# Byte offsets of split weight tiles by kind of product, and a reordered start, in a two-block float32 model on one core

## The chip, the cores and the metric

The kernel runs on one NeuronCore of a Trainium2 chip. The metric is the device time of one execution in microseconds; lower is better. Before the change the median of three runs is 3207.17 us (3205.44 to 3207.61).

## What is computed

Two transformer-like blocks of width 1024 follow each other, each with two layers, in float32. The first block carries 256 latent and 256 context tokens; its layers hold two half-step swiglus and a mixer, Fourier in the first and retention in the second, and every part is modulated by shifts, scales and gates that are products of a condition vector with `ada_w`. The second block carries the 256 latent tokens alone, with a mixer of gated recurrences and attention. Cut to what matters:

```
def swiglu(h, w_gate, w_up, w_down):
    return (jax.nn.silu(h @ w_gate) * (h @ w_up)) @ w_down
def half_ffn(t, m, j):
    h = modulate(rmsnorm(t, norm_g[l, j]), m[3 * j], m[3 * j + 1])
    return t + 0.5 * m[3 * j + 2] * swiglu(h, ffn_w_gate[l, j // 2], ffn_w_up[l, j // 2], ffn_w_down[l, j // 2])
x = half_ffn(x, m_lat, 0)
h_lat = modulate(rmsnorm(x, norm_g[l, 1]), m_lat[3], m_lat[4])
x = x + m_lat[5] * y_lat
x = half_ffn(x, m_lat, 2)
```

The hidden width of a swiglu is 2816. In the second block a layer is x + 0.5 swiglu, x + mixer, x + 0.5 swiglu, and the mixer's input product has 10752 columns. In the last layer of the first block only the latent tokens are needed behind retention.

## The kernel before

**Split products.** A float32 product is made of three products of rounded parts: every operand is split into a high part (type fp32r) and a low part, and `mm3` (L272 to L274) issues high by high, high by low, low by high into one PSUM tile. Activations are kept split in SBUF (class `Split`, tiles `s`); weights are split as they arrive.

**Requests for weights.** Every use of a weight piece is one call of `get` or `getw` (L205, L222), a *request*. A first pass over the whole program with dummies writes the list of requests, the plan; the second pass emits instructions and looks ahead in that plan. `pump` (L176) issues the DMA of a request up to four requests ahead on SP (`_dma`, L150, into one of four `raw` buffers) and then its split (`_split`, L158): ScalarE copies the piece to `wh` (L166), VectorE makes `wl` = raw - `wh` (L167), both in tiles of a pool with three buffers. The subtraction is put off into `subs` and emitted at the next `tick`, or at the latest when its request is asked for. A piece has up to 2048 columns per partition: 8 k tiles of 256 columns, 4 of 512, or fewer.

**Offsets.** A `wh` or `wl` buffer is 512 bytes longer than its piece. Where `odd` is set, the tile starts at a byte offset that rotates with the number i of the request in the plan, the same for `wh` and `wl`:

```
o = OFFSETS[i % len(OFFSETS)] // 4 if odd else 0
```

with the 16 values 0, 4, 8, 12, 16, 20, 24, 28, 32, 40, 48, 56, 64, 96, 128 and 192. `odd` is set behind the first three swiglus, so retention and all that follows rotates, and what stands ahead has offset 0. Raw requests (`ada_n`, `ada_t`) count in i but are not split.

**Kinds of product.** The first two and a half layers multiply with 512 columns moving (both streams, `ffn2s`, L592), except each swiglu's first gate and up request, its last four k tiles (`by_stream`, L663) and the Fourier layer, which go stream by stream with 256 columns. Behind that nearly all have 256 columns moving and the weights stationary (`gemm_t`, L566): swiglus (`ffn`, L691), retention's q and gates, the mixers' transposed units (`unit_t`, L1223). Retention's k requests move 512 columns. The swiglu behind retention moves 258 in gate and up (`shift`). In `gemm_n` (L583) the activations are stationary and the weights move, 256 columns: retention's v and the mixers' `unit_n` (L1234).

**The order on the engines** is the order in which the Python code emits; nothing reorders it later. In the mixers, `tick` (L226) puts steps of attention and recurrence chains between the products.

**The start** (L1721 to L1746). `consts` (L360) loads vectors, the identity and the two halves of x on ScalarE's queue. `ada_first` (L392) makes the first shift and scale on TensorE from two times four raw chunks of `ada_n`. `sums` gathers squares of x (ScalarE L477, VectorE L483), `rstd` turns them into 1/rms, `lead` (L541) scales x by it, and `lead_end` (L551) applies scale and shift and splits: ScalarE L556 for the high part, VectorE L558 and L560 for the low. The first weight request stands before the last raw chunk. The first gate request runs on the latent half k tile by k tile, two output tiles each, with all three products at once (`pair_t`, L574, `early` 2).

Of the kernel before, what the change touches and what calls it, by code (L numbers as in the profile page):

```python
# [10 lines left out]
F32R = mybir.dt.float32r  # L11
# [8 lines left out]
KT = 8  # L20
# [8 lines left out]
LATE = 9  # L29
SCRATCH = 1024  # L30
GAP = 2048 - SCRATCH - 128
OFFSETS = (0, 4, 8, 12, 16, 20, 24, 28, 32, 40, 48, 56, 64, 96, 128, 192)
PAD = 512

# [55 lines left out]
class Ker:  # L90
    def __init__(self, tc, I, out, plan):
# [17 lines left out]
        self.uid = 0  # L109
        self.quiet = False  # L110
        self.splim = None
        self.odd = False

# [44 lines left out]
    def _split(self, i):  # L158
        src, raw, odd = self.plan[i]
# [5 lines left out]
        wl = self.wsp.tile([128, 2048 + PAD // 4], F32R, name="wl", tag="wl")[:, o:]  # L165
# [38 lines left out]

    def get(self, src, raw=False):  # L205
        self.asked.append((src, raw, self.odd))
# [4 lines left out]
        assert self.plan[i] == (src, raw, self.odd) or str(self.plan[i]) == str((src, raw, self.odd))  # L211
# [10 lines left out]
    def getw(self, w, k0, k1, c0, c1):  # L222
        return self.get(w.rearrange("(k p) m -> p k m", p=128)[:, k0:k1, c0:c1])

# [134 lines left out]
class Model(Ker):  # L359
    def consts(self):  # L360
# [10 lines left out]
        nc.scalar.dma_start(self.x[:, :, CTX], xv[:, :, CTX])  # L371
        self.late[LATE] = self.ada_begin
# [199 lines left out]


    def pair_t(self, ps, u, X, c, early):  # L574
        cut = [(k, k + 1) for k in range(KT)] if early == 2 else [(0, 6), (6, KT)] if early else [(0, KT)]
        for k0, k1 in cut:
# [15 lines left out]
    def ffn2s(self, H, wg, wu, wd, gate, g_next, mid=None, late=(0, 1, 4), first=None):  # L592
# [3 lines left out]
        def up(f0, f1):  # L596
            G = Gs[f0] = Split(self, f1 - f0, N1)
            for f in range(f0, f1, 2):
                ug = first if first and f == 0 else self.getw(wg, 0, KT, 128 * f, 128 * f + 256)
                pg = [self.mm() for _ in range(2)]  # L600
                if f == 0:
# [3 lines left out]
                    for c in STREAM:  # L605
                        for u, p in ((ug, pg), (uu, pu)):
                            for m in self.pair_t([p[m][:, c] for m in range(2)], u, H, c, 2 if first and u is ug and c == LAT else 0):
                                self.tick()
# [11 lines left out]
                uu = self.getw(wu, 0, KT, 128 * f, 128 * f + 256)  # L620
                for m in range(2):
# [6 lines left out]
        def down(f0, f1):  # L628
            G = Gs[f0]
            ks = ((f0, f0 + 5), (f0 + 5, f1)) if f1 - f0 > 8 else ((f0, f1),)  # L630
            for mp in range(4):
                pd = [self.mm() for _ in range(2)]
                for k0, k1 in ks:
                    u = self.getw(wd, k0, k1, 256 * mp, 256 * mp + 256)
                    for m in range(2):
# [55 lines left out]
    def ffn(self, X, wg, wu, wd, resid, after=None, shift=False):  # L691
        n = N2 + 2 if shift else N2
        cx, c = slice(0, n), slice(0, N2)
        for hi, (f0, f1) in enumerate(self.HALVES):
            G = Split(self, f1 - f0, N2)
            for f in range(f0, f1, 2):
                ug = self.getw(wg, 0, KT, 128 * f, 128 * f + 256)
# [3 lines left out]
                uu = self.getw(wu, 0, KT, 128 * f, 128 * f + 256)  # L701
                pu = [self.mm([128, n]) for _ in range(2)]
# [213 lines left out]
    def retention(self, H, before, after):  # L916
# [21 lines left out]
        for hd in range(4):  # L938
# [27 lines left out]
            uk = self.getw(wi, 0, KT, 1024 + 256 * hd, 1280 + 256 * hd)  # L966
            pk = [self.mm() for _ in range(2)]
# [745 lines left out]
def body(M, stop):  # L1713
# [15 lines left out]

    def load():  # L1730
        M.splim = LATE - 1
        first.append(M.getw(I["ffn_w_gate"][0, 0], 0, KT, 0, 256))
    H = Split(M, KT, N1)
    M.splim = LATE - 2
# [34 lines left out]

    M.odd = True  # L1770
    M.retention(H, lambda: M.shifted_begin(2), M.pre)
# [62 lines left out]
```

## Time and profile before

| | |
|---|---|
| median of three runs | 3207.17 us |
| the profiled execution's own time | 3207.72 us |
| its span | 3205.9 us |
| TensorE products busy | 3165.0 us, 99% |
| VectorE busy | 2192.3 us, 68% |
| ScalarE busy | 1367.3 us, 43% |
| DMA | 510.69 MB, mean 159 GB/s |

The rows further down come from this one execution. Times are microseconds from the start of the span; a row of a stretch gives its limits, its length, then for each engine the busy time and the number of instructions in it, the granted share of TensorE's clock (1.00 is 2.4 GHz) and what the DMA moved.

### The profile page before, as it was taken

The page shows a single profiled execution, that of the slowest core. Times are in us where ns is not written, and L with a number is a line of the kernel's source. Part 1 is how long each engine was busy: PE and PEld are TensorE (multiplying, and loading weights), DVE is VectorE, ACT ScalarE, POOL GpSimd, SP SyncE. Part 2 cuts the span into 40 slices and gives each one's busy share as a digit, 9 for nine tenths or more (in the row PEclk, how much of TensorE's full clock was granted, in tenths as well). Part 3 has the DMA queues.
Part 4 walks back from the last instruction along what each step waited for, and adds up shares of the span by engine and source line. Part 5 has one row for each costly group of instructions (what it writes and reads, how often), then busy time and mean ns, then how long its engine had stood idle before and what let it go on. Part 6 is the DMA issues. An engine that isn't in the chain of part 4 may idle for free.

```text
span 3205.9 us, 53822 instructions
## 1 busy us (share of the span) xinstructions
PE 3165.0 (99%) x22520; PEld 2968.3 (93%) x22520; DVE 2192.3 (68%) x4077; ACT 1367.3 (43%) x1945; POOL 0.5 (0%) x5
## 2 busy tenths in 40 slices
PE   7999999999999999999999999999999999999999
PEld 5888898888988889999999999999999999999999
DVE  6797578874666537666757568767757568876755
ACT  3222353222322225444445456654544446655543
POOL 0000000000000000000000000000000000000000
PEclk9999999999999999999999999999999999999999
DMA  7465413554256532333555554444565555444563
GB/s 266 168 220 181 140 54 132 184 197 131 80 175 218 170 103 94 118 113 124 166 178 194 186 176 158 146 144 132 191 191 185 183 172 175 145 147 142 172 195 122
DMA packets 431699, 510.69 MB, mean 159 GB/s; under 512 B 8800, under 2 KB 396128, under 8 KB 431456
## 3 DMA queue, kind: packets, MB, share of 16 engines
q1 hardware_dynamic: 426656, 501.25, 47.5%
q10 hardware_dynamic: 4800, 5.99, 0.6%
q8 instruction: 177, 2.90, 0.4%
q14 instruction: 66, 0.54, 0.0%
HBM read 506.16 MB, written 1.05 MB: 158 GB/s over the span
## 4 chain that ended last, share of the span: by engine, by line
PE 92%; DVE 5%; ACT 1%; DMA 1%; issue 1%; ACTq 0%; DVEq 0%
PE mm L272 30%; PE mm L274 29%; PE mm L273 29%; PE mm L1450 2%; DVE wl L167 1%; DMA x<-in_xT 1%; DVE x L658 1%; PE mm L1609 1%; DVE s L523 0%; PE aux L1659 0%; PE mm L1593 0%; DVE s L520 0%; DVE sqs L483 0%; PE mm L1641 0%; ACT wh L166 0%
## 5 line engine op out<-in xcount | busy, mean ns | idle before, releaser
L272 PE MATMUL mm<-s,wh 128*128 128x256 f32 (+2 forms) x5888 | 1829.3, 311 | 4.4 <-ACT s L521 2.5
L273 PE MATMUL mm<-s,wh 128*128 128x256 f32 (+2 forms) x5888 | 1820.8, 309 | 2.5 <-DVE s L1337 0.7
L274 PE MATMUL mm<-s,wl 128*128 128x256 f32 (+2 forms) x5888 | 1819.6, 309 | 2.3 <-DVE wl L167 2.3
L272 PEld LDWEIGHTS mm<-s,wh 128*128 128x128 f32 x5888 | 1114.7, 189 | 63.9 <-ACT s L521 3.7
L273 PEld LDWEIGHTS mm<-s,wh 128*128 128x128 f32 x5888 | 1114.5, 189 | 63.6 <-DVE s L523 3.9
L274 PEld LDWEIGHTS mm<-s,wl 128*128 128x128 f32 x5888 | 1114.4, 189 | 61.6 <-DVE wl L167 3.9
L167 DVE TENSOR_TENSOR wl<-raw,wh 128x2048 fp32r<-128x2048 f32 (+2 forms) x438 | 929.0, 2123 | 244.0 <-ACT wh L166 244.0
L166 ACT ACTIVATE wh<-raw 128x2048 fp32r<-128x2048 f32 (+2 forms) x438 | 776.3, 1778 | 612.9 <-PE mm L273 224.9
L457 DVE SCALAR_TENSOR_TENSOR jk<-raw,s 128x512 bf16<-128x512 f32 x448 | 309.0, 690 | 12.2
L272 PE MATMUL mm<-wh,s 128*128 128x256 f32 x960 | 275.8, 287 | 0.0
L273 PE MATMUL mm<-wl,s 128*128 128x256 f32 x960 | 269.9, 281 | 0.0
L274 PE MATMUL mm<-wh,s 128*128 128x256 f32 x960 | 269.9, 281 | 0.0
L752 ACT ACTIVATE s<-tmp 128x256 fp32r<-128x256 f32 (+1 forms) x176 | 87.8, 499 | 423.2 <-DVE tmp L738 319.6
L273 PEld LDWEIGHTS mm<-wl,s 128*128 128x128 f32 x960 | 181.9, 189 | 0.2
L272 PEld LDWEIGHTS mm<-wh,s 128*128 128x128 f32 x960 | 181.6, 189 | 0.3
L274 PEld LDWEIGHTS mm<-wh,s 128*128 128x128 f32 x960 | 181.6, 189 | 0.0
L738 DVE TENSOR_TENSOR tmp<-tmp,mm 128x512 f32<-128x512 f32 x66 | 45.2, 685 | 195.8 <-PE mm L274 158.7
L658 DVE SCALAR_TENSOR_TENSOR x<-mm,cm,x 128x256 f32<-128x256 f32 x160 | 71.8, 478 | 105.5 <-PE mm L274 105.5
L750 DVE TENSOR_TENSOR tmp<-mm,sqs 128x256 f32<-128x256 f32 x88 | 36.8, 418 | 83.1 <-PE mm L274 83.1
L754 DVE TENSOR_TENSOR s<-tmp,s 128x256 fp32r<-128x256 f32 (+1 forms) x176 | 91.3, 519 | 2.2 <-ACT s L752 1.1
L749 ACT ACTIVATE tmp<-tmp 128x256 f32<-128x256 f32 x88 | 36.2, 411 | 102.8 <-DVE tmp L748 102.8
L483 DVE TENSOR_TENSOR sqs<-sqs,tmp 128x256 f32<-128x256 f32 x119 | 49.8, 418 | 25.7 <-ACT tmp L477 24.6
(243 smaller groups left out, 1988.8 us busy)
## 6 DMA issues: line engine op xcount, KB each, us to landing
raw<-in_ffn_w_in SPq DMA_DIRECT2D x88, 1024.0 KB, 4.9
raw<-in_w_in SPq DMA_DIRECT2D x84, 1024.0 KB, 4.8
raw<-in_ada_t SPq DMA_DIRECT2D x64, 1024.0 KB, 5.3
raw<-in_ffn_w_gate SPq DMA_DIRECT2D x44, 1024.0 KB, 5.2
raw<-in_ffn_w_up SPq DMA_DIRECT2D x44, 1024.0 KB, 5.2
raw<-in_ret_w_in SPq DMA_DIRECT2D x24, 1024.0 KB, 4.9
raw<-in_ffn_w_out SPq DMA_DIRECT2D x32, 768.0 KB, 4.6
raw<-in_ffn_w_down SPq DMA_DIRECT2D x32, 640.0 KB, 4.0
```

What stands on the lines that cost most here:

```text
L166: self.A.activation(wh[:, :n], t[:, :n], AF.Copy)
L167: self.subs.append((i, lambda: self.V.tensor_sub(wl[:, :n], t[:, :n], wh[:, :n].bitcast(F32))))
L272: T.matmul(ps, ah, bh, start=first, stop=False)
L273: T.matmul(ps, ah, bl, start=False, stop=False)
L274: T.matmul(ps, al, bh, start=False, stop=last)
L457: V.scalar_tensor_tensor(jk, r[:, j, 512 * i:512 * i + 512], 1.0, self.cb[s][i], OP.mult, OP.mult, accum_out=a[:, 2 * q + j, s, i:i + 1])
L483: self.defer(lambda: self.V.tensor_add(sqs, sqs, q))
L658: self.V.scalar_tensor_tensor(self.x[:, d, e], ps[:, e.start - c.start:e.stop - c.start], gate(d, s), self.x[:, d, e], OP.mult, OP.add)
L738: V.tensor_mul(g, sg, pu)
L752: A.activation(G.h(f), g, AF.Copy)
L754: self.defer(lambda: V.tensor_sub(G.l(f), g, G.h(f).bitcast(F32)))
L1450: T.matmul(ps[:m, a, b], kc, qc, start=True, stop=True)
```

## The change

The rotation and the flag `odd` go. Each request names its offset: `NARROW` (64 bytes) is the default of `getw`, `WIDE` (0) is given where 512 columns move, `MOVING` (192) in the mixers' `unit_n`; retention's v keeps the default. The gate and up requests of the swiglu behind retention take the 22 values of `SHIFTED` in turn. The early layers' narrow requests so change from 0 to 64. The buffers are as long as before.

At the start, x is loaded on SP ahead of the chunks, in the order latent, context. The sums and scalings of both halves move between the chunks of `ada_n` (`latent` and the other hooks), the first weight request comes behind the last chunk, and its low part is not emitted when it is asked for (`lazy`), but by `catch_up` behind `lead_end`. Its latent half runs in three passes over all k tiles, high by high, high by low, low by high (`pair_first`). The core of the diff:

```
-        o = OFFSETS[i % len(OFFSETS)] // 4 if odd else 0
-        wh = self.wsp.tile([128, 2048 + PAD // 4], F32R, name="wh", tag="wh")[:, o:]
+        wh = self.wsp.tile([128, 2048 + PAD // 4], F32R, name="wh", tag="wh")[:, at // 4:]
...
+WIDE, NARROW, MOVING, PAD = 0, 64, 192, 512
+SHIFTED = (12, 68, 72, 76, 80, 84, 52, 44, 204, 200, 208, 196, 140, 136, 132, 144, 40, 36, 100, 88, 160, 176)
...
+    def getw(self, w, k0, k1, c0, c1, at=NARROW):
...
-        if self.subs and self.subs[0][0] <= i:
+        if self.subs and self.subs[0][0] <= i and not self.lazy:
...
-        nc.scalar.dma_start(self.x[:, :, LAT], xv[:, :, LAT])
+        for c in STREAM:
+            nc.sync.dma_start(self.x[:, :, c], xv[:, :, c])
...
+    def pair_first(self, ps, u, X, c):
+        wh, wl = u
+        for i in range(3):
+            for k in range(KT):
+                x = (X.l if i == 1 else X.h)(k, c.start, c.stop)
+                for m in range(2):
+                    self.T.matmul(ps[m], (wh, wh, wl)[i][:, k, 128 * m:128 * m + 128], x,
+                                  start=i == 0 and k == 0, stop=i == 2 and k == KT - 1)
...
+                at = (SHIFTED[f], SHIFTED[f + 1]) if shift else (NARROW, NARROW)
...
-        u = self.getw(self.w_in, 0, KT, c, c + 256)
+        u = self.getw(self.w_in, 0, KT, c, c + 256, MOVING)
...
-    M.ada_first(0)
-    r.append(M.rstd(LAT))
-    sums(1)
-    M.ada_first(1, {2: lambda: xr.append(M.lead(0, r[0])), 4: lambda: r.append(M.rstd(CTX)), 6: load})
+    def latent():
+        xr.append(M.lead(0, r[0]))
+        sums(1)
+    M.ada_first(0, {2: lambda: r.append(M.rstd(LAT)), 4: latent})
+    M.ada_first(1, {0: lambda: r.append(M.rstd(CTX)), 4: lambda: xr.append(M.lead(1, r[1]))})
+    M.splim = LATE
+    M.lazy = True
+    first.append(M.getw(I["ffn_w_gate"][0, 0], 0, KT, 0, 256))
+    M.lazy = False
...
-    xr.append(M.lead(1, r[1]))
```

The offsets move no instruction. The order changes at the start alone. On SP, the first issues before (`raw` is a weight or chunk buffer):

```order
L155 DMA raw<-in_ada_n 128x2x1024 x7
L155 DMA raw<-in_ffn_w_gate 128x8x256
L155 DMA raw<-in_ada_n 128x2x1024
L155 DMA raw<-in_ffn_w_up 128x8x256
L432 DMA s_1_91<-in_c_row 128x512
```

and now:

```order
L369 DMA x<-in_xT 128x8x256 x2
L156 DMA raw<-in_ada_n 128x2x1024 x8
L156 DMA raw<-in_ffn_w_gate 128x8x256
L156 DMA raw<-in_ffn_w_up 128x8x256
L432 DMA s_1_92<-in_c_row 128x512
```

Both halves of x come ahead of all chunks, and the gate weights behind the eighth.

On TensorE, up to the first products (L401 chunks of ada, eight products a pair of k tiles; L408 and L498 transposes; L489 the sums of squares over partitions), before:

```order
L401 MATMUL aux<-raw,s_5_104 32x256 x32
L408 MATMUL aux<-ident,tmp 128x128 x2
L489 MATMUL aux<-oD,sqs 128x1 x2
L401 MATMUL aux<-raw,s_5_104 32x256 x8
L498 MATMUL aux<-ident,nw 128x128 x2
L401 MATMUL aux<-raw,s_5_104 32x256 x8
L489 MATMUL aux<-oD,sqs 128x1 x2
L401 MATMUL aux<-raw,s_5_104 32x256 x16
L408 MATMUL aux<-ident,tmp 128x128 x2
L498 MATMUL aux<-ident,nw 128x128 x2
L272 MATMUL mm<-s_6_108,wh 128x256
L273 MATMUL mm<-s_14_116,wh 128x256
```

and now:

```order
L401 MATMUL aux<-raw,s_5_104 32x256 x8
L489 MATMUL aux<-oD,sqs 128x1 x2
L401 MATMUL aux<-raw,s_5_104 32x256 x8
L498 MATMUL aux<-ident,nw 128x128 x2
L401 MATMUL aux<-raw,s_5_104 32x256 x16
L408 MATMUL aux<-ident,tmp 128x128 x2
L489 MATMUL aux<-oD,sqs 128x1 x2
L401 MATMUL aux<-raw,s_5_104 32x256 x16
L498 MATMUL aux<-ident,nw 128x128 x2
L401 MATMUL aux<-raw,s_5_104 32x256 x16
L408 MATMUL aux<-ident,tmp 128x128 x2
L580 MATMUL mm<-s_6_108,wh 128x256 x2
```

The sums of both halves and both transposes of 1/rms now stand between the chunks; nothing but the last transpose of the shift and scale stands between the last chunk and the first product.

On VectorE, the end of the latent half's low parts (`s_20` and `s_21` are two of them) and what follows, in the changed kernel:

```order
L560 TENSOR_TENSOR s_20_122<-tmp,s_12_114 128x256
L560 TENSOR_TENSOR s_21_123<-tmp,s_13_115 128x256
L167 TENSOR_TENSOR wl<-raw,wh 128x2048 x2
L558 TENSOR_SCALAR tmp<-s_26_293,ca,mod 128x256 x2
L560 TENSOR_TENSOR s_14_116<-tmp,s_6_108 128x256
```

Before, the first `wl` stood ahead of the latent half's sixteen operations; now both `wl` come behind them and ahead of the context half's.

## Rows read from the trace of the kernel before

**Rows 1.** The page, parts 1 and 4: whole span; chain that ended last.

```profile
PE 3165.0 (99%) x22520; PEld 2968.3 (93%) x22520; DVE 2192.3 (68%) x4077; ACT 1367.3 (43%) x1945; POOL 0.5 (0%) x5
...
PE 92%; DVE 5%; ACT 1%; DMA 1%; issue 1%; ACTq 0%; DVEq 0%
```

**Rows 2.** Windows of one narrow request each, offsets 64, 96, 0 and 28.

```profile
2373.53:2378.97 5.44, 5.44 (x50) 5.44 (x49) 3.66 (x4) 1.92 (x1) 0.00 (x0) 1.00 0.63 202
2378.97:2384.74 5.77, 5.77 (x51) 5.77 (x50) 2.58 (x3) 2.64 (x3) 0.00 (x0) 1.00 0.55 184
2396.08:2401.83 5.75, 5.75 (x50) 5.75 (x49) 3.58 (x6) 2.64 (x3) 0.00 (x0) 1.00 0.55 185
2510.38:2516.78 6.40, 6.40 (x50) 6.40 (x49) 4.07 (x6) 2.64 (x3) 0.00 (x0) 1.00 0.41 124
```

**Rows 3.** Windows, weights moving: mixer at 192 and 0, retention v at 64.

```profile
1976.60:1979.10 2.50, 2.50 (x23) 2.50 (x23) 1.89 (x6) 2.43 (x7) 0.00 (x0) 1.00 0.51 142
1983.86:1986.49 2.63, 2.63 (x23) 2.63 (x23) 2.60 (x9) 2.56 (x7) 0.00 (x0) 1.00 0.47 141
1257.70:1268.59 10.89, 10.89 (x98) 10.88 (x97) 8.66 (x13) 4.96 (x9) 0.00 (x0) 1.00 0.30 97
```

**Rows 4.** Windows of one request with 512 columns, offsets 0, 56 and 28.

```profile
208.67:219.55 10.88, 10.88 (x49) 9.01 (x48) 9.17 (x21) 1.92 (x1) 0.00 (x0) 1.00 0.69 242
1246.52:1257.70 11.18, 11.18 (x50) 9.01 (x49) 7.30 (x13) 7.76 (x12) 0.00 (x0) 1.00 0.31 103
1368.52:1381.30 12.78, 12.78 (x51) 9.22 (x50) 5.57 (x10) 2.43 (x2) 0.00 (x0) 1.00 0.64 204
```

**Rows 5.** Windows of two whole swiglus of the second block.

```profile
2271.03:2458.49 187.46, 187.46 (x1593) 187.46 (x1591) 120.59 (x169) 87.59 (x99) 0.00 (x0) 1.00 0.58 185
2458.49:2649.34 190.85, 190.85 (x1593) 190.85 (x1592) 120.98 (x171) 86.76 (x100) 0.00 (x0) 1.00 0.57 183
```

**Rows 6.** Windows, 258 columns: at 40 (45 products), at 12 (48).

```profile
1528.25:1533.80 5.55, 5.55 (x47) 5.55 (x47) 5.20 (x13) 1.00 (x1) 0.00 (x0) 1.00 0.67 196
1585.92:1591.53 5.61, 5.61 (x50) 5.61 (x49) 3.29 (x8) 2.42 (x3) 0.00 (x0) 1.00 0.45 140
```

**Rows 7.** Windows, 512 weight columns: output projection at 64, by stream at 0.

```profile
1427.30:1430.00 2.70, 2.70 (x25) 2.70 (x24) 2.35 (x13) 0.00 (x0) 0.00 (x0) 1.00 0.62 169
388.50:394.25 5.75, 5.75 (x50) 5.75 (x49) 3.60 (x9) 4.11 (x12) 0.00 (x0) 1.00 0.52 175
```

**Rows 8.** Timeline of the start: start, length (us), engine, line, operation [idle before].

```profile
28.85 0.42 ACT L477 ACTIVATE sqs<-x 128x256 f32<-128x256 f32 x1 [5.30 <-DMA x<-in_xT]
...
36.46 3.47 PE L401 MATMUL aux<-raw,s 128*32 128x256 f32 x32
...
38.61 2.29 DVE L167 TENSOR_TENSOR wl<-raw,wh 128x2048 fp32r<-128x2048 f32 x1
...
41.33 4.05 ACT L556 ACTIVATE s<-s,mod,ca 128x256 fp32r<-128x256 f32 x8 [0.94 <-DVE ca L422]
...
41.98 0.39 PE L272 MATMUL mm<-s,wh 128*128 128x256 f32 x1 [0.88 <-ACT s L556]
...
45.93 0.75 DVE L560 TENSOR_TENSOR s<-tmp,s 128x256 fp32r<-128x256 f32 x2
...
49.67 0.28 PE L272 MATMUL mm<-s,wh 128*128 128x256 f32 x1
...
66.95 0.40 PE L272 MATMUL mm<-s,wh 128*128 128x512 f32 x1
```

**Rows 9.** Windows of the start.

```profile
0.00:5.00 5.00, 0.00 (x0) 0.00 (x0) 0.12 (x3) 0.00 (x0) 0.52 (x5) 1.00 0.60 160
20.00:25.00 5.00, 0.69 (x2) 0.29 (x2) 3.12 (x9) 3.05 (x9) 0.00 (x0) 1.00 1.04 413
35.00:40.00 5.00, 4.39 (x36) 2.31 (x36) 3.49 (x14) 0.00 (x0) 0.00 (x0) 0.54 0.80 264
```

**Rows 10.** Window in the first mixer where VectorE is busiest.

```profile
2040.00:2060.00 20.00, 20.00 (x173) 20.00 (x172) 19.04 (x24) 13.14 (x37) 0.00 (x0) 1.00 0.48 159
```

More of the change, by code (lines that the diff above doesn't have):

```diff
@@ L110, in __init__ @@
         self.quiet = False
+        self.lazy = False
         self.splim = None
-        self.odd = False
     def pools(self, ctx):
@@ L158, in _split @@
     def _split(self, i):
-        src, raw, odd = self.plan[i]
+        src, raw, at = self.plan[i]
         if raw:
@@ L162, in _split @@
         t, v, n = self.rawt.pop(i)
-        o = OFFSETS[i % len(OFFSETS)] // 4 if odd else 0
-        wh = self.wsp.tile([128, 2048 + PAD // 4], F32R, name="wh", tag="wh")[:, o:]
-        wl = self.wsp.tile([128, 2048 + PAD // 4], F32R, name="wl", tag="wl")[:, o:]
+        wh = self.wsp.tile([128, 2048 + PAD // 4], F32R, name="wh", tag="wh")[:, at // 4:]
+        wl = self.wsp.tile([128, 2048 + PAD // 4], F32R, name="wl", tag="wl")[:, at // 4:]
         self.A.activation(wh[:, :n], t[:, :n], AF.Copy)
@@ L203, in catch_up, with get @@
             self.flush_subs()
-    def get(self, src, raw=False):
-        self.asked.append((src, raw, self.odd))
+    def get(self, src, raw=False, at=WIDE):
+        self.asked.append((src, raw, at))
         i = self.nget
@@ L210, in get @@
             return (self.nc, self.nc) if not raw else self.nc
-        assert self.plan[i] == (src, raw, self.odd) or str(self.plan[i]) == str((src, raw, self.odd))
+        assert self.plan[i][1:] == (raw, at) and (self.plan[i][0] == src or str(self.plan[i][0]) == str(src))
         if not raw:
@@ L220, in get @@
         return self.splt.pop(i)
-    def getw(self, w, k0, k1, c0, c1):
-        return self.get(w.rearrange("(k p) m -> p k m", p=128)[:, k0:k1, c0:c1])
+    def getw(self, w, k0, k1, c0, c1, at=NARROW):
+        return self.get(w.rearrange("(k p) m -> p k m", p=128)[:, k0:k1, c0:c1], at=at)
     def tick(self):
@@ L571, in gemm_t @@
                      X.l(k - j0, c.start, c.stop), first and k == k0, last and k == k1 - 1)
+    def pair_first(self, ps, u, X, c):
[6 more added lines that the diff above has]
+                                  start=i == 0 and k == 0, stop=i == 2 and k == KT - 1)
+        yield from range(2)
     def pair_t(self, ps, u, X, c, early):
-        cut = [(k, k + 1) for k in range(KT)] if early == 2 else [(0, 6), (6, KT)] if early else [(0, KT)]
+        cut = [(0, 6), (6, KT)] if early else [(0, KT)]
         for k0, k1 in cut:
@@ L598, in up @@
             for f in range(f0, f1, 2):
-                ug = first if first and f == 0 else self.getw(wg, 0, KT, 128 * f, 128 * f + 256)
+                at = WIDE if f else NARROW
+                ug = first if first and f == 0 else self.getw(wg, 0, KT, 128 * f, 128 * f + 256, at)
                 pg = [self.mm() for _ in range(2)]
@@ L606, in up @@
                         for u, p in ((ug, pg), (uu, pu)):
-                            for m in self.pair_t([p[m][:, c] for m in range(2)], u, H, c, 2 if first and u is ug and c == LAT else 0):
+                            pp = [p[m][:, c] for m in range(2)]
+                            lead = first and u is ug and c == LAT
+                            for m in self.pair_first(pp, u, H, c) if lead else self.pair_t(pp, u, H, c, False):
                                 self.tick()
@@ L619, in up @@
                     self.tick()
-                uu = self.getw(wu, 0, KT, 128 * f, 128 * f + 256)
+                uu = self.getw(wu, 0, KT, 128 * f, 128 * f + 256, WIDE)
                 for m in range(2):
@@ L633, in down @@
                 for k0, k1 in ks:
-                    u = self.getw(wd, k0, k1, 256 * mp, 256 * mp + 256)
+                    u = self.getw(wd, k0, k1, 256 * mp, 256 * mp + 256, WIDE)
                     for m in range(2):
@@ L700, in ffn @@
                     self.tick()
-                uu = self.getw(wu, 0, KT, 128 * f, 128 * f + 256)
+                uu = self.getw(wu, 0, KT, 128 * f, 128 * f + 256, at[1])
                 pu = [self.mm([128, n]) for _ in range(2)]
@@ L965, in retention @@
                 ml, mc = self.ret_mask(0)
-            uk = self.getw(wi, 0, KT, 1024 + 256 * hd, 1280 + 256 * hd)
+            uk = self.getw(wi, 0, KT, 1024 + 256 * hd, 1280 + 256 * hd, WIDE)
             pk = [self.mm() for _ in range(2)]
@@ L1728, in sums @@
             M.stat(d, STREAM[s])
-    def load():
-        M.splim = LATE - 1
-        first.append(M.getw(I["ffn_w_gate"][0, 0], 0, KT, 0, 256))
     H = Split(M, KT, N1)
-    M.splim = LATE - 2
+    M.splim = LATE - 1
     sums(0)
-    M.ada_first(0)
-    r.append(M.rstd(LAT))
-    sums(1)
-    M.ada_first(1, {2: lambda: xr.append(M.lead(0, r[0])), 4: lambda: r.append(M.rstd(CTX)), 6: load})
+    def latent():
[7 more added lines that the diff above has]
+    M.lazy = False
     M.rel(M.sc32)
@@ L1768, in body @@
         return dump()
-    M.odd = True
     M.retention(H, lambda: M.shifted_begin(2), M.pre)
```

5 lines of the change are left out of this document (1 added, 4 removed).

## The prediction

> **What bounds the kernel now.** I read the page first. TensorE is busy 99% of the span and holds 92% of the chain that ended last; VectorE has 5% of that chain, everything else 1% each [rows 1]. So outside the first 50 us a stage is as long as its products on TensorE are apart, and the question is what sets that distance. I then cut the span into windows that run from the first product of one weight request to the first of the next. Each such window holds 48 products (2 output tiles, 8 k tiles, 3 products each; the counts in the rows show 2 or 3 more, since a product's modelled end overlaps the next window), so its length over 48 is the distance from start to start. TensorE is busy throughout these windows at a granted clock of 1.00, its higher level of 2.4 GHz: there is no wait in them.
>
> Four requests of the same kind (weights stationary, 256 columns moving) that differ in nothing but the offset of their split tiles give 5.44 us at 64 bytes, 5.77 at 96, 5.75 at 0 and 6.40 at 28 [rows 2]: 113.3, 120.2, 119.8 and 133.3 ns a product. Read the same way over the whole program, a kind's distance repeats by offset to within a nanosecond in most places: with stationary weights, and in the retention's v, 64 bytes gave 113 to 114 ns in 14 of its 15 requests (256 columns). The offset of before rotates through 16 values, so a stage pays their mean, about 118.4 ns, and the first three swiglus with the Fourier layer always have offset 0. I read every number below as such a distance.
>
> With the weights moving in the mixers, 22 starts took 2.50 us at 192 bytes and 2.63 at 0 [rows 3]: 113.6 against 119.5 ns. In the retention's v requests (96 products, weights moving too) 64 bytes took 10.89 us, 113.4 ns [rows 3]. With 512 columns a request took 10.88 us at offset 0, 11.18 at 56 and 12.78 at 28 [rows 4], 226.7 ns against 232.9 and 266.
>
> **The change part by part.** The number of instructions, their shapes and the buffers stay; each split tile only starts elsewhere, so ScalarE, VectorE and DMA do the same work. What falls is the distance between products.
>
> *Swiglus of the second block.* Each makes 1584 products (22 gate and up requests of 48, 16 down requests of 36 or 30); at 113.5 ns that is 179.8 us. The one in windows without a slow offset lasts 187.46 us, the one that meets offsets 28 and 32 in its gate and up requests 190.85 [rows 5]. I leave 0.9 us of each for the norm's small products at its start. That gives 6.8 and 10.1 us; two of each kind make **34 us**.
> *Narrow requests of the two mixers* (48 with 256 columns of weights): 2304 products from a mean of 118.4 to 113.6: **11.1 us**. Their *moving requests*: 44, 2112 products, mean 118.5 to 113.9, since some products behind a chain instruction start late: **9.6 us**.
> *Retention*: v, 768 products from 119.4 to 113.4, 4.6 us; q and gates, 576 from 118.4 to 113.5, 2.8 us (64 was never used there, but at 8 and 12 bytes these requests read as the swiglus do); its four wide k requests from 12.78, 11.18 and two between 10.88 and 11.18 back to 10.88, 2.5 us. Sum **9.9 us**.
> *Down products of the swiglu behind it*: 528 from 118.6 to 113.5, **2.7 us**.
> *That swiglu's gate and up* have 258 columns and get a table of 22 offsets, of which before shows only 12 and 40 there. They read 116.9 ns (5.61 us for 48) at 12 and 123.3 (5.55 us for 45) at 40 [rows 6]; the mean of all 22 was 120.1. A value 4 bytes away can differ by some ns either way, so I price the table at that mean: **0 us**, with ends of 113.5 and 123.4 ns, -7 and +3.5 us.
> *Requests of 512 weight columns in steps of four k tiles* (output projections, branches, by stream, Fourier). The only one at 64 bytes ran 23 starts in 2.70 us, 117.4 ns, once a chain instruction had come between, after 12 at 113.4; a by-stream request at 0 takes 5.75 us for 48 [rows 7]. At 117: 960 early products from 119.8, 2.7 us, and 960 later from 118.0, 1.0 us. Ends 113.5 and 120. Together **3.7 us**.
> *First gate and up of the three early swiglus*: 576 products, 120.0 to 113.6, **3.7 us**.
>
> *The start.* Before, the second half of x lands at 28.85 us behind seven chunks of ada weights; its sum of squares stands ahead of the last chunks in TensorE's order, which run at 36.46; the first product starts at 41.98, the up request at 49.67, the third request at 66.95 [rows 8]. Now SP issues x first. The queue moves 0.8 MB by 5 us and then 413 GB/s [rows 9], so x (2.1 MB) is there by 9 us, the last of eight chunks (10.7 MB with the constants) at 29, the gate weights at 31.5. TensorE's in-order list of sums, chunks and transposes ends near 33; the split of wh, some 2 us (wl's pass over as many elements took 2.29), now stands before the shifted tiles on ScalarE, so the first product starts near 35.6, six before. But its second pass waits for the low parts on VectorE, 16 operations that took 5.35 us (41.33 to 46.68), and its third for wl, 2.29 us, now behind them [rows 8]. That puts the third pass at 43.0, its 16 products at 120 to 240 ns end at 45 to 46.9, against 49.67 (the granted clock averaged 0.54 from 35 to 40, largely its lower level of 1.2 GHz, while chunks came in bursts [rows 9]). I take **4 us**; ends 6.4 (the first product's whole lead) and 0. The context half needs 5.35 us of VectorE behind the up split (45.3) and is ready at 50.6, just before the up request ends; if it is a microsecond later, TensorE waits.
>
> Sum: 34 + 11.1 + 9.6 + 9.9 + 2.7 + 3.7 + 3.7 + 4 = 78.7 us. The profiled execution took 3207.72 us, 0.55 above the median of the three runs; from the median that leaves **3128.5 us**.
>
> The Trainium skill speaks against all but the start: by "TensorE: Matmul & The Clock Gate", section "Wait — 56ns, not 53.3ns?", products that follow each other start N / 2.4 GHz and some 2.5 ns apart, by estimate from that page 109 ns for 256 columns wherever they lie, and by "Step-by-step: what each phase is for" the weights load through a read port of their own. By that rule the sum would be the 4 us alone. The trace does not agree: 113.3 and 133.3 ns stand at the same clock.
>
> **The rivals.** *VectorE takes part of it back in the mixers.* There it is up to 19.04 of 20 us busy [rows 10], and its work does not shrink. If it becomes the bound in the half of the mixers where it is above 85%, half of their 20.7 us stay: 3139. Against it: PE shows no wait in that window. Chance 0.11.
> *64 bytes meets a slow partner.* 28 bytes is slow only in gate and up of the first swiglu of each second-block layer; elsewhere it runs at 117. So the moving tile's place counts as well, and 64 was never seen in those 44 requests. If they run at 133.3: 2112 products by 19.8 ns, 41.8 us less gain, 3170. For 64 speak gate requests of the other swiglus at 113.4. Chance 0.06.
> *Slower than before*: the same partner effect is the rule for gate, up and down, because all three rotating buffers now carry one offset, and the requests read at 64 stood between others at other offsets. Each product at 133.3 instead of 113.5 costs 19.8 ns; the whole gain is gone from 4000 of them on, 84 requests. Over the 7920 products of the five 256-token swiglus it costs 157 us of the forecast, 3285. Against it stand the 14 requests at 64, whose 48 products ran at one distance from the first to the last, whatever the neighbours. Chance 0.03.
> *The offset is not the cause*, and the 16 steps only happen to fall on kinds of request: the start alone remains, 3203. Against it: 64 bytes reads 113 to 114 in gate, up, down and v alike. Chance 0.04. This is also what the Trainium skill's page named above would give.
>
> **The numbers.** The forecast has 0.76. Its own ends are the table (-7, +3.5), the requests of 512 weight columns (-6, +5.6) and the start (-2.4, +4): 3113 to 3142 if all fall one way, which I cut to 3114 below. With the VectorE rival and some of these ends on top of it the range is **3114 to 3146**; the cases outside have 0.13. About 0.2%, 6.4 us, is what a measurement can tell from no change. Faster by more: forecast, VectorE and slow-partner cases, 0.93; within: 0.04; slower: 0.03.
>
> **What would show it.** In the profile after, every narrow request of the second block should last 5.45 us, moving stretches 113 to 114 ns a start, all wide requests 10.88; a swiglu stage about 181 us, and the third request should start near 62 us. A gate request of a first swiglu at 6.4 us, waits of TensorE for VectorE in the mixers of more than some 3 us each, or narrow requests still between 116 and 120 ns would prove it wrong.

## The result, and the profile after

| | |
|---|---|
| before | 3207.22 us (3205.44 to 3207.61, 4 runs) |
| changed | 3163.03 us (3161.63 to 3168.05, 4 runs) |
| ratio | 0.9866, 95% interval 0.9849 to 0.9883 |
| forecast | 3128.5 us, range 3114 to 3146 |

The change saves 44 us where 79 were forecast. The profiled execution took 3162.56 us, its span 3160.8. Engine rows of the page, then the first line of the chain that ended last, as in [rows 1]:

```profile
PE 3121.8 (99%) x22520; PEld 2928.3 (93%) x22520; DVE 2192.4 (69%) x4077; ACT 1368.3 (43%) x1945; POOL 0.5 (0%) x5
...
PE 92%; DVE 5%; ACT 1%; issue 1%; DMA 1%; SPq 0%; ACTq 0%; DVEq 0%
```

TensorE is still busy 99% of the span, so what is missing must lie in the distance between products. Windows as in [rows 2 to 5]: a gate request of the second swiglu of layer 0 and an up request of the first of layer 1, both at 64 bytes; these two swiglus as a whole, all at 64; a wide k request; 95 starts of retention's v at 64; 22 starts each of two mixer requests at 192.

```profile
2345.08:2350.73 5.65, 5.65 (x50) 5.65 (x49) 3.67 (x4) 1.92 (x1) 0.00 (x0) 1.00 0.63 202
2479.73:2485.17 5.44, 5.44 (x51) 5.44 (x49) 4.18 (x6) 2.65 (x3) 0.00 (x0) 1.00 0.44 143
2242.84:2429.88 187.04, 187.04 (x1592) 187.04 (x1591) 120.69 (x169) 87.59 (x99) 0.00 (x0) 1.00 0.57 186
2429.88:2610.29 180.41, 180.41 (x1593) 180.41 (x1591) 120.46 (x169) 86.80 (x100) 0.00 (x0) 1.00 0.59 193
1238.08:1248.98 10.90, 10.90 (x50) 9.01 (x49) 7.37 (x14) 7.48 (x12) 0.00 (x0) 1.00 0.33 112
1248.98:1260.17 11.19, 11.19 (x96) 11.18 (x95) 8.43 (x12) 5.37 (x9) 0.00 (x0) 1.00 0.31 97
1953.30:1955.89 2.59, 2.59 (x24) 2.59 (x24) 2.50 (x6) 2.53 (x7) 0.00 (x0) 1.00 0.27 76
1957.02:1959.51 2.49, 2.49 (x23) 2.49 (x23) 2.46 (x5) 0.72 (x2) 0.00 (x0) 1.00 0.48 171
```

The same offset now gives two lengths. 5.65 us for 48 products is 117.7 ns, 5.44 is 113.3. One whole swiglu lies at the one value, the next at the other, at the same granted clock. The first of these two requests is the one that stands at 64 in [rows 2] too, and read 5.44 us there: same weights, same products, same offset. The load beside them is not what differs: over the two whole swiglus VectorE is busy 120.69 and 120.46 us and DMA moves 186 and 193 GB/s. The v request reads 117.8 ns; at the same offset it read 113.4 in [rows 3]. At 192 the moving weights read 117.7 and 113.2.

Where does the distance change? The timeline of TensorE at the start of the slow swiglu shows the only foreign products between its requests, and windows of 4 us ahead of the first break and behind the second follow:

```profile
2247.60 0.50 PE L489 MATMUL aux<-oD,sqs 128*128 128x1 f32 x4
2254.41 0.38 PE L498 MATMUL aux<-ident,nw 128*128 128x128 f32 x2
```

```profile
2243.00:2247.00 4.00, 4.00 (x38) 4.00 (x37) 2.72 (x6) 3.50 (x4) 0.00 (x0) 1.00 0.61 214
2256.00:2260.00 4.00, 4.00 (x36) 4.00 (x35) 1.85 (x5) 3.01 (x6) 0.00 (x0) 1.00 1.05 373
```

Ahead of the norm's sum (L489) 38 products overlap the window, behind it 36. From start to start that is 113.3 ns in the stretch ahead of L489, and 117.8 in the 54 products between the two breaks and in the 1529 behind the second, which run on into the next swiglu; they do not fall back. The 1529 behind the last break of the first swiglu of layer 1 stand at 113.3 throughout. I call a product that is not of the three products of a split a **break**, and what lies between two breaks a **stretch**. Nearly every stretch with 256 columns, weights stationary or moving, settles within some five products at one of these two values and keeps it.

The kernel before had shown the slow value at 64 too, in the mixers' moving requests, behind breaks. The first of four:

```profile
1955.09:1960.51 5.42, 5.42 (x47) 5.42 (x47) 4.31 (x12) 2.74 (x4) 0.00 (x0) 1.00 0.61 193
```

These 46 starts lie 117.8 ns apart, and the other three requests read the same. The prediction's count of requests at 64 took in stationary weights and retention's v alone.

The start, as in [rows 8]:

```profile
33.68 1.91 ACT L166 ACTIVATE wh<-raw 128x2048 fp32r<-128x2048 f32 x1 [0.98 <-DMA raw<-in_ffn_w_gate]
...
36.13 7.20 PE L580 MATMUL mm<-s,wh 128*128 128x256 f32 x32 [2.94 <-ACT s L556]
...
40.74 4.48 DVE L167 TENSOR_TENSOR wl<-raw,wh 128x2048 fp32r<-128x2048 f32 x2
...
43.17 2.00 PE L580 MATMUL mm<-s,wl 128*128 128x256 f32 x16
...
45.01 0.28 PE L272 MATMUL mm<-s,wh 128*128 128x256 f32 x1
...
61.49 0.40 PE L272 MATMUL mm<-s,wh 128*128 128x512 f32 x1
```

First product at 36.13 (forecast 35.6), third pass at 43.17 (43.0), up request at 45.01 (45 to 46.9), third request at 61.49 (62). This part went as worked out.

### The profile page after: what moved, and what is told of

Its sections match the earlier page's. It is cut to its first block, busy times and chain, and to the rows that moved or that the text cites. A ratio compares the mean times of both kernels' runs of the same rounds, so it can differ in the third digit from the quotient of the medians.

```text
span 3160.8 us, 53819 instructions
## 1 busy us (share of the span) xinstructions
PE 3121.8 (99%) x22520; PEld 2928.3 (93%) x22520; DVE 2192.4 (69%) x4077; ACT 1368.3 (43%) x1945; POOL 0.5 (0%) x5
## 4 chain that ended last, share of the span: by engine, by line
PE 92%; DVE 5%; ACT 1%; issue 1%; DMA 1%; SPq 0%; ACTq 0%; DVEq 0%
PE mm L272 29%; PE mm L274 29%; PE mm L273 29%; PE mm L1465 2%; DVE wl L167 1%; ACT wh L166 1%; DVE x L672 1%; PE mm L1624 1%; DVE s L523 0%; DMA raw<-in_ada_n 0%; PE aux L1674 0%; PE mm L1608 0%; DVE s L520 0%; DVE sqs L483 0%; PE mm L580 0%
## 5 line engine op out<-in xcount | busy, mean ns | idle before, releaser
L772 DVE SCALAR_TENSOR_TENSOR x<-mm,x 128x256 f32<-128x256 f32 x64 | 27.0, 423 | 53.9 <-PE mm L274 53.7
```

## The experiments

**1. The same kernel again, and its two parts alone.** `again` is the changed kernel unedited. `offs_only` has its offsets on the start of before. `start_only` has its start with the rotation of before:

```
         src, raw, at = self.plan[i]
+        at = (0, 4, 8, 12, 16, 20, 24, 28, 32, 40, 48, 56, 64, 96, 128, 192)[i % 16] if i >= 184 else 0
```

> The changed kernel as it is, a second look at it. Theory (two settled distances at one offset, 113.3 and 117.8 ns; which of them a stretch gets is decided by the instants at which it restarts behind other work on TensorE, and it holds until the next such break): the states are not drawn by chance but follow from the program's timing, so the swiglus of the second block read as in the first profile, first swiglu of a layer fast, second slow, in total 3160 to 3168 us; where one swiglu falls differently the time moves by 1584 x 4.5 ns = 7 us. Rival (the state is drawn by chance at every restart): other swiglus are slow than before, and runs are spread over 3145 to 3175 us. Rival (the place of the moving tiles makes the second swiglu slow): always as in the first profile.

> Offsets as changed, the start as before. By the account of the two traces the start is worth some 5 us, so 3207 - 45 + 5 = 3168 us. Theory of two settled distances: stretches may restart at other instants, so single swiglus may change between 180 and 187 us; each is worth 7 us. Rival (the distance is fixed by offset, neighbours and place alone): the same distances as in the changed kernel in every stage.

> The start as changed, offsets rotating as before. The third request starts some 5 us earlier and nothing else changes: 3202 us. My prediction's term for the start was 4 us, with ends 0 and 6.4: 3203 us. Theory of two settled distances: with 16 offsets in turn each request re-enters from another distance, so the later stages stay as before within 1 us. If single requests change their distance although nothing but the time of their start moved, the instant of entry matters there as well.

`again`: 3162.39 us, ratio 0.9857 (0.9841 to 0.9874). The four swiglus stand as in the first profile. Of 187 stretches from retention on, 177 settle at the same of the two values in both profiles. So the value is not drawn by chance at every break: most of it follows from the program. It is not wholly fixed by it either: single executions, 3168.05 us of the changed kernel and 3156.87 of `kick56`, lie some 5 to 6 us above the others of their kernel, about what one swiglu is worth.

`offs_only`: 3168.55 us, 0.9876 (0.9861 to 0.9891). Its four swiglus read like those of the changed kernel. `start_only`: 3203.36 us against 3208.22 on the same chip, 0.9984 (0.9975 to 0.9994), so 4.9 us. In the profile of `offs_only` the third request starts at

```profile
66.32 0.40 PE L272 MATMUL mm<-s,wh 128*128 128x512 f32 x1
```

so 4.8 of the 5.5 us by which it comes earlier than in [rows 8] are the new order. In the profiled execution of `start_only` (3206.31 us; two of its ten took that long, the others 3201.61 to 3204.20) some later requests read otherwise than before at the same offset, although only their time had moved. First retention's v request of [rows 3], at 64; then the last narrow request of the first mixer, at 28, here and in the kernel before:

```profile
1253.01:1264.20 11.19, 11.19 (x96) 11.19 (x95) 8.74 (x13) 5.17 (x9) 0.00 (x0) 1.00 0.29 94
2261.10:2267.50 6.40, 6.40 (x51) 6.40 (x50) 4.42 (x7) 1.64 (x4) 0.00 (x0) 1.00 0.60 199
...
2265.43:2271.03 5.60, 5.60 (x50) 5.60 (x49) 4.42 (x7) 1.63 (x4) 0.00 (x0) 1.00 0.52 172
```

The v request stands at 117.8 ns (95 starts), where [rows 3] read 113.4; the one at 28 at 133.3, where it read 116.7. That costs 0.8 us in each layer, and the next request, the first of the second swiglu, 0.6 more: the expected 1 us was exceeded. These losses come to 2.8 us, about what this execution lies above the other eight, so in those the requests may have read as before. Either way a reading at one offset of the rotation changed where nothing but instants had moved.

**2. An odd request in the slow stage.** `kick56`:

```
-                at = ... if shift else (NARROW, NARROW)
+                at = ... if shift else (56 if f == 2 else NARROW, NARROW)
```

> The changed kernel, but the third request of each second-block swiglu (gate of tiles 2 and 3, behind the last break of the stage) at 56 bytes instead of 64. In the kernel before, a request at 64 that followed one at 56 without a break read 113 to 114 ns in every case. Theory (two settled distances, the change of offset lets it settle anew): the second swiglus of both layers run at 113.3 from the fourth request on, 1480 products x 4.5 ns = 6.6 us less each, the first swiglus pay 0.2 us each for the 56: about 3150 us. Rival (neighbouring buffers at the same offset make it slow): only the requests next to the 56 gain, 0.4 us: 3163. Rival (the place of the moving tiles of the second swiglu): 3163.

3150.86 us, 0.9824 (0.9809 to 0.9839). Windows of the second swiglu of layer 0: the request at 56, the next one at 64, the whole stage.

```profile
2255.78:2261.51 5.73, 5.73 (x52) 5.73 (x50) 2.97 (x8) 4.45 (x7) 0.00 (x0) 1.00 0.98 344
2261.51:2266.95 5.44, 5.44 (x50) 5.44 (x49) 4.52 (x6) 3.33 (x4) 0.00 (x0) 1.00 0.22 67
...
2243.89:2424.72 180.83, 180.83 (x1593) 180.83 (x1592) 120.20 (x168) 87.64 (x99) 0.00 (x0) 1.00 0.59 192
```

180.83 us, where 187.04 stood: in the stage only the weight tiles of that one request are in another place, so neither the moving tiles of that swiglu nor neighbours at one offset make it slow. All four swiglus now stand at 113.3 behind the request at 56; their gain is 33.6 us against before (10.0, 6.6, 10.2, 6.8), close to the 34 of the forecast.

**3. More breaks.** `breaks` puts a transpose into a spare tile ahead of four gate requests of each of these swiglus:

```
                 ug = self.getw(wg, 0, KT, 128 * f, 128 * f + 256, at[0])
+                if f in (4, 8, 14, 18) and not shift:
+                    self.T.transpose(self.aux([128, 128]), self.ident, self.ident)
```

> The changed kernel with four foreign products more in each second-block swiglu: a transpose of the identity into a spare PSUM tile, whose result nobody reads, ahead of the gate requests of tiles 4, 8, 14 and 18 (0.1 to 0.4 us each of extra work). Theory (two settled distances at 64 bytes; a break lets it settle anew, and it holds until the next break): inside one swiglu whole stretches between the transposes now read 113.3 or 117.8 ns, with changes at the transposes only, and at least one of the 16 stretches behind them differs from the first profile's 113.3, 117.8, 113.3, 117.8 for the four swiglus. Rival (only a change of offset lets it settle anew, a break does not matter): each swiglu keeps its distance through all four transposes.

3166.28 us in one execution. The second swiglu of layer 0: its four transposes in the timeline, then windows between the transposes, of 20, 20, 19 and 20 us.

```profile
2269.73 0.27 PE L714 MATMUL aux<-ident 128*128 128x128 f32 x1
...
2292.46 0.27 PE L714 MATMUL aux<-ident 128*128 128x128 f32 x1
...
2357.87 0.27 PE L714 MATMUL aux<-ident 128*128 128x128 f32 x1
...
2379.77 0.27 PE L714 MATMUL aux<-ident 128*128 128x128 f32 x1
```

```profile
2272.00:2292.00 20.00, 20.00 (x173) 20.00 (x172) 12.69 (x18) 10.15 (x11) 0.00 (x0) 1.00 0.62 198
2296.00:2316.00 20.00, 20.00 (x179) 20.00 (x178) 13.40 (x19) 8.46 (x11) 0.00 (x0) 1.00 0.44 143
2360.00:2379.00 19.00, 19.00 (x170) 19.00 (x170) 11.80 (x17) 9.96 (x11) 0.00 (x0) 1.00 0.58 196
2382.00:2402.00 20.00, 20.00 (x172) 20.00 (x171) 11.67 (x18) 8.86 (x11) 0.00 (x0) 1.00 0.42 132
```

173, 179, 170 in 19 us, 172: slow, fast, fast, slow. In all four swiglus the value changes at breaks and nowhere between. A break alone, with no change of offset, re-decides.

**4. All offsets in rising order.** `screen_both` gives the 152 requests of the four swiglus the offsets 0, 4, ... 508 and on from 0, `screen_low` the same to the low tile alone, the high one at 64:

```
+        ah = al = at
+        if at == NARROW and i in SWI:
+            ah, al = (4 * SWI[i] % 512,) * 2        # screen_low: 64, 4 * SWI[i] % 512
```

> The changed kernel, but the 152 requests of the four second-block swiglus take the offsets 0, 4, 8, ... 508 in rising order (and then from 0 again), the same for both tiles of a request. Theory (an offset has one or two settled distances): between 113.3 and 133.3 ns a request, with 64 at 113.3 behind 60 if entry from another offset lets it settle fast, values that recur with the period of the address pattern (the same at o and o + 256, perhaps at o + 64 or o + 128), and a mean of about 118.4, as the 16 rotating values had: the four stages together near the 727 to 753 us of before. Rival (64 alone is a good place, whatever stands ahead): only 64 below 115.

> The changed kernel, but in the 152 requests of the four second-block swiglus the high tile stays at 64 bytes and the low tile takes 0, 4, 8, ... 508 in rising order. If the distance of a product hangs on its own weight tile alone, the two products with the high tile stay at 113.3 or 117.8 ns and only the third moves, between 113 and 133. If it is one rhythm of the stream of products, all three move together. If an offset of the low tile keeps the whole at 113.3 in every stage, it is a candidate for all narrow requests.

`screen_both`: 3181.16 us in one execution. Requests at 28, 32, 36 and 40 in the first swiglu of layer 0 (48 products each), and at 24, 28 and 32 in the second swiglu of layer 1 (48 each):

```profile
1741.62:1748.02 6.40, 6.40 (x51) 6.40 (x49) 4.35 (x6) 2.64 (x3) 0.00 (x0) 1.00 0.39 123
1748.02:1754.42 6.40, 6.40 (x51) 6.40 (x49) 4.24 (x7) 2.64 (x3) 0.00 (x0) 1.00 0.40 125
1754.42:1760.82 6.40, 6.40 (x51) 6.40 (x50) 3.20 (x5) 2.64 (x3) 0.00 (x0) 1.00 0.38 123
1760.82:1766.53 5.71, 5.71 (x51) 5.71 (x50) 3.96 (x7) 2.22 (x3) 0.00 (x0) 1.00 0.46 138
...
3091.20:3096.89 5.69, 5.69 (x51) 5.69 (x49) 3.68 (x4) 1.93 (x1) 0.00 (x0) 1.00 0.63 202
3096.89:3102.49 5.60, 5.60 (x50) 5.60 (x49) 2.49 (x3) 2.64 (x3) 0.00 (x0) 1.00 0.52 179
3102.49:3108.17 5.68, 5.68 (x50) 5.68 (x49) 3.56 (x6) 2.65 (x3) 0.00 (x0) 1.00 0.55 185
```

28, 32 and 36 read 133.3 ns in the first place, 28 and 32 read 116.7 and 118.3 in the second. So the 133.3 of [rows 2] and [rows 5] was no property of 28 either, and a value can be handed on over two changes of offset. 64, 52, 76 and 88 read 113.4 to 114.1 on entry from the offset 4 below (76 once 120.0), and 8 read 116.1 in the one request there without a break (means of whole requests, with their first products). `screen_low` (3174.53 us, one execution): the two products with the high tile change with the low tile's offset, by the product starts 113 to 121 ns at an unchanged 64 bytes (means of requests behind the first two of each swiglu). It is one rhythm of the stream, not a price of each tile.

**5. An offset with one value.** `narrow8` has `NARROW = 8`.

> The changed kernel with 8 bytes instead of 64 for all narrow requests (stationary weights and the retention's v). In the kernel before, 8 bytes read 115.5 to 115.9 ns in all 18 stationary stretches, behind breaks and behind requests at 4, so it looks like an offset with one settled distance. Then all narrow stationary requests of the later layers read 115.6 (now 115.9 in the mean of 113.3 and 117.8), the v requests some 120 (8 moving read 120.0): 3160 to 3166 us, with all four swiglus at the same 183 us. If uniform use brings out a second distance at 8 too, the swiglus differ from each other.

3161.25 us, 0.9858 (0.9841 to 0.9874), its four executions within 0.8 us. The second swiglu of layer 0 and the first of layer 1:

```profile
2244.43:2428.16 183.73, 183.73 (x1593) 183.73 (x1591) 120.46 (x168) 87.48 (x99) 0.00 (x0) 1.00 0.57 189
2428.16:2611.92 183.76, 183.76 (x1592) 183.76 (x1591) 120.88 (x170) 86.78 (x100) 0.00 (x0) 1.00 0.58 190
```

Of its 107 stationary stretches of at least 12 products behind the early layers 103 read 115.5 to 116.1, behind whatever break; the other four, of 12 products each, read 116.7. That is one value where 64 had two. As a total it equals 64 with its two.

**6. Other offsets, with breaks.** `uniform` keeps the transposes of `breaks` and gives whole stages 88, 52, or two values for the two tiles.

> The four transposes a swiglu of the run breaks, so that each stage restarts often, and other offsets, one for a whole stage: 88 in the first swiglu of layer 0, in the down products behind retention and in the narrow requests of that layer's mixer; 52 in the second swiglu of layer 0, in the mixer of layer 1 and in retention's narrow requests; 64 for the high and 88 for the low tile in the first swiglu of layer 1; 64 and 76 in its second; moving requests at 88 (layer 0) and 204 (layer 1), the v requests at 192, 88, 52 and 76. These were the values that read 113.3 to 114 ns on every entry from another offset in the two runs with rising offsets. Theory (two settled distances, drawn at each break): most of these have a slow distance as well, and the stretches behind the breaks of a stage divide between 113.3 and some 118 to 120 ns. An offset that has one distance alone, at 113.3 to 114 behind every break, would be the better choice; 8 bytes, one distance at 115.6, shows that there are such offsets. Rival (a few good offsets keep 113.3 however they are entered, and 64 is just not one of them): all stretches of 88 and 52 at 113.3 to 114.

3171.35 us in one execution. The first swiglu of layer 0 at 88, windows in three stretches:

```profile
1723.00:1743.00 20.00, 20.00 (x169) 20.00 (x169) 14.00 (x20) 10.17 (x12) 0.00 (x0) 1.00 0.66 219
1746.00:1766.00 20.00, 20.00 (x179) 20.00 (x178) 12.29 (x19) 9.62 (x12) 0.00 (x0) 1.00 0.52 159
1812.00:1832.00 20.00, 20.00 (x169) 20.00 (x168) 11.71 (x17) 10.14 (x11) 0.00 (x0) 1.00 0.59 190
```

120.0, 113.3, 120.0 ns: 88 has both, and so has 52; the pair 64 and 76 has 113.3 and 117.8. The pair 64 and 88 stood at 117.8 in every stretch of its swiglu. None is fast however it is entered; the rival fell.

**7. Putting it together.** `kicks_and_8` takes the request at 56, also ahead of each half of the down products behind retention, 8 bytes in the early layers and in retention's narrow requests, 192 for v, and

```
+SHIFTED = (12, 12, 8) + (12,) * 9 + (8,) + (12,) * 9
```

> The changed kernel with the parts that the runs so far speak for: the request at 56 bytes behind the last break of each second-block swiglu (as in the run kick56, 3150.9 us there), the same ahead of each half of the down products behind retention (528 products from 117.8 to 113.3 less two requests at 56: 2.2 us); 8 bytes, the offset with one distance of 115.6, for the narrow requests that breaks cut into short stretches in the early layers and in retention (1.0 us early, 1.0 in retention by the stages of the run narrow8); retention's v requests at 192 (117.8 now, half of the stretches at 113.3 in the mixers: 1.7 us); and the swiglu behind retention at 12 bytes throughout, entered from 8 in each half (12 read 116.7 ns with 258 columns in the kernel before, both times behind 8, and 120.0 now behind 64: 1056 products, up to 3.5 us). Theory of two settled distances: 3150.9 - 2.2 - 2.0 - 1.7 - 3.5 = 3141.5 us. If the gains of kick56 hang on that program's timing alone rather than on the entry from another offset, swiglus fall back to 187 us, 6.6 us each, and it stays above 3145.

3141.67 us, 0.9796 (0.9782 to 0.981); four executions took 3141.16 to 3142.09, the profiled one 3147.53. In that one the first swiglu of layer 0 is slow:

```profile
1690.44:1880.38 189.94, 188.42 (x1598) 187.93 (x1597) 127.90 (x197) 87.80 (x102) 0.00 (x0) 1.00 0.55 183
2240.45:2421.09 180.64, 180.64 (x1592) 180.64 (x1591) 120.14 (x168) 87.62 (x99) 0.00 (x0) 1.00 0.59 192
```

(183.38 us in the changed kernel's profile.) Behind the request at 56 the first half of the down products behind retention stands at 113.3, the second at 117.8. So 56 does not always help, and two more runs asked why. Both move the odd request two further on (`f == 4`), where no break stands next to it; `kick56_late` keeps 56, `kick8_late` takes 8 there and in the down products.

> The kernel of the run kicks_and_8 with the request at 56 bytes moved from the third to the fifth request of each second-block swiglu. In that run's profile the third request of layer 0's first swiglu is itself cut by a break, and the stretch behind it settled at 117.8 (one swiglu, 6.4 us; its profiled execution took 3147.5, the other four 3141 to 3142); the down products behind the second half behind retention settled at 117.8 too. Theory (entry from 56 lands at 113.3 in most cases, not in all): 96 more products of each stage stay as the last break left them, up to 0.4 us each; 3140.5 to 3143 us, with fewer executions 6 us above the rest, if it was the break inside the request that spoilt the entry; if it is chance of the entry, single executions near 3147 remain.

> As kick56_late, but the odd request is at 8 bytes, where the distance settled at 115.6 behind every break and every entry. Theory (what decides is the rhythm from which 64 is entered): from 8 that rhythm is always the same, so the four swiglus behind the odd request and the two groups of down products settle all alike, all at 113.3 (3140 us, and no execution 6 us above) or all at 117.8 (3140 + 4 x 6.3 + 1.5 = 3167 us). If they divide, 8 is entered and left in more than one rhythm in spite of its one mean distance.

`kick56_late` took 3154.73 us, 0.9843 (0.983 to 0.9857): 13 more, not 1 less; its profiled execution took 3161.82 us, the other three some 7 us less. In that profile, the request ahead of the odd one, the odd one and the whole second swiglu of layer 0:

```profile
2258.59:2264.24 5.65, 5.65 (x50) 5.65 (x49) 4.72 (x6) 3.32 (x4) 0.00 (x0) 1.00 0.24 80
2264.24:2269.90 5.66, 5.66 (x51) 5.66 (x50) 3.49 (x6) 2.64 (x3) 0.00 (x0) 1.00 0.84 292
...
2240.97:2428.19 187.22, 187.22 (x1593) 187.22 (x1592) 120.67 (x169) 87.56 (x99) 0.00 (x0) 1.00 0.56 185
```

`kick8_late`, the request ahead, the one at 8, the next, and the stage:

```profile
2251.66:2257.31 5.65, 5.65 (x50) 5.65 (x49) 4.73 (x6) 3.32 (x4) 0.00 (x0) 1.00 0.23 79
2257.31:2262.86 5.55, 5.55 (x50) 5.55 (x49) 3.37 (x6) 2.65 (x3) 0.00 (x0) 1.00 0.87 300
2262.86:2268.30 5.44, 5.44 (x50) 5.44 (x49) 4.28 (x6) 2.65 (x3) 0.00 (x0) 1.00 0.51 172
...
2234.22:2415.18 180.96, 180.96 (x1592) 180.96 (x1591) 120.13 (x168) 87.51 (x99) 0.00 (x0) 1.00 0.58 192
```

With 56 and no break, the stage goes on as it was: in the profile three swiglus stayed at 117.8, one at 113.3. With 8 all four swiglus, three of which came in at 117.8, and both groups of down products go on at 113.3; the five executions lie within 1.7 us (3142.50 us, 0.9801, 0.9787 to 0.9814). So my reading of experiment 2 was right in the gain and wrong in its reason: 56 alone hands on what it meets. In experiment 2 the request at 56 stood right behind a break in three swiglus and had a break inside it in the fourth, so I take it that the stretch was decided anew with 56 in it. The runs fit that (all six swiglus of `kick56` and `kicks_and_8` where the break stands right ahead went on at 113.3, of the two with the break inside one), but none tries it by itself. 8, which has one value itself, wipes out the difference.

## Why the prediction was wrong

By the starts of requests in both traces, against the terms of the sum:

| stretch of the program | forecast gain, us | measured, us |
|---|---|---|
| up to retention (start 4, first gate and up 3.7, early 512-column 2.7) | 10.4 | 8.4 |
| retention (9.9, and output projections 0.4) | 10.3 | 4.1 |
| swiglu behind it (table 0, down 2.7) | 2.7 | -0.1 |
| four second-block swiglus | 34 | 21.4 |
| two mixers (11.1, 9.6, branches 0.6) | 21.3 | 11.4 |
| sum | 78.7 | 45.2 |

The spans differ by 45.1.

- **The step that failed** is the first one: "a kind's distance repeats by offset to within a nanosecond in most places", and with it the 113.5 ns put on every narrow request. What repeats is a pair of values, 113.3 and 117.8 at 64; which one holds is decided at a break and then kept. With 16 offsets in turn, almost every request of a swiglu entered from another rhythm, and at 64 that always led to 113.3; but in the rotation 64 always follows 56, and 56 follows 48, so it was one entry over and over. With one offset throughout, whatever the break left stays for 1500 products. The 14 of 15 requests were not 14 tries at the new situation, and the count left out the four moving requests of the mixers at 64, all at 117.8. That their 48 products "ran at one distance from the first to the last, whatever the neighbours" said nothing of a neighbour at 64.
- **The swiglus.** Two gained 10.13 and 10.44 us, where 10.1 each was forecast; the size is right. The other two gained 0.4 instead of 6.8 each: they settled at 117.8, and the mean over the stage fell by 0.1 ns only.
- **The mixers** stand at 113.3 and 117.8 in turn, on average at 115.3 (moving) and 115.6 (narrow) instead of 113.9 and 113.6. **Retention** settles at 117.8 nearly throughout, v and the gates alike; the wide k requests gave their 2.3 of 2.5 us. The **down products** behind it stand at 117.8 as well.
- **The table** was worth 0, as priced (-0.4 with its restarts): mean 120.1 ns before and after. 12 read 120.0 there instead of the 116.9 of [rows 6]; entered from 8 it read 116.7 again in `kicks_and_8`. So the table shares the trait.
- **The first gate and up of the early swiglus** gave 1.5 us of 3.7: 0.6 in the first, which is what the third request's lead of 5.5 us holds beyond the 4.8 of the order, and 0.9 in the other two, where the products settle at 113.3 in one and at 117.8 in the other.
- **The requests of 512 weight columns** gave 2.9 of 3.7 us by the starts of their products, 1.8 of 2.7 early and 1.1 of 1.0 behind. [rows 7] showed 113.4 and then, behind a break, 117.4, and I put that down to the kind of request. It was the trait itself, on view in one row. That 28 reads 133.3 in one stage and 117 in others, named under the rivals, was a second sign of it, and I kept it as a small chance of a slow partner.
- **The start** gave 4.9 us against 4, by the steps forecast.
- **The rivals.** VectorE took back little in the mixers: in the first TensorE stood idle for 2.7 us, where it had stood idle for 2.2. The slow partner in the first swiglus did not come; their gate and up stand at 113.3. That the offset is no cause falls with `narrow8`, where a change of offset alone brings the second swiglu of layer 0 and the first of layer 1, at 117.8 and 113.3 with 64, to the same 115.6. The Trainium skill, in "TensorE: Matmul & The Clock Gate", section "Wait — 56ns, not 53.3ns?", gives by estimate 109 ns for 256 columns and no term for where the tiles lie; no settled stretch of any run here was below 113.3, at a granted clock of 1.00.

**What stays open.** What, at a break, decides between the two values: the outcome mostly repeats between executions, and I found no field of the trace that tells it ahead of the stretch. The first two starts of a stretch tell part of it. In the changed kernel's profile, from retention on, the 25 stretches of at least 12 products whose first two starts lie 205 to 207 ns apart all settle at 113.3, and so do all 24 in `again`; those with 200 to 203 ns divide, 47 at 113.3 and 87 at 117.8. So the outcome is in part visible by the second product; what sets it was not tried. Which read meets which in the slow rhythm was not tried.

## What to carry to other kernels

A distance between products read from a mixed stream belongs to that stream, not to the address alone; before putting one address everywhere, ask what set the state in the sample, and look for stretches of the same address with another value. Exceptions in a reading that is otherwise exact (one of 15, or a value that changes behind a break) are worth more than the 14 that fit. Where a stage settles badly, one odd request whose own distance never varies can reset it: 48 products at 115.6 instead of 113.3 cost 0.1 us and brought 6 in each stage that had settled slow.

## What was not expected of the hardware

Back-to-back products of one shape keep one of two distances, 113.3 or 117.8 ns, over more than 1500 products and 30 requests with three buffers in rotation, while VectorE, ScalarE and DMA do different work beside them. A single foreign product of 0.27 us can switch it. 8 bytes has one value (115.5 to 116.1) with stationary weights, 64, 52 and 88 have two or more, and 28 has 116.7 and 133.3. The best version here, at 3141.67 us 21 below the changed kernel, differs from it in offsets alone.
